# Wide weight loads for the small experts of a top-2-of-8 expert layer, and another order of the first loads

## The chip, the cores and the metric

The kernel runs on one core of one Trainium2 chip. Its time is the device time of one execution in microseconds, of the slowest core (here the only one): 1435.9 us is the median of three runs (1432.8 to 1438.07).

## The reference

A trunk of two layers over 256 tokens of 1024 columns, in float32. Each layer has three groups of attention heads beside each other (a 2-D neighbourhood, a dilated mixture, a fixed memory of 256 rows), an output projection and a channel mixer: a dense SwiGLU in layer 0, eight experts with the best two per token in layer 1.

```python
D_MODEL, SEQ, MEM_LEN = 1024, 256, 256
D_FF, N_EXPERTS, TOP_K, D_FF_EXPERT = 2816, 8, 2, 3584

def swiglu(x, w_gate, w_up, w_down):
    return (jax.nn.silu(x @ w_gate) * (x @ w_up)) @ w_down

# moe_swiglu, in short: each token goes through the two experts with the largest logits,
# and their results are added, weighted by a softmax over the two logits
logits = x @ w_router
top_logit, top_idx = lax.top_k(logits, TOP_K)
gates = jax.nn.softmax(top_logit, axis=-1)
y[token] += gate * swiglu(x[token], w_gate[e], w_up[e], w_down[e])
```

An expert has 29.36 MB of gate and up weights (1024 rows of 3584 columns each) and 14.68 MB of down weights (3584 rows of 1024 columns). All eight are read, whatever the routing.

## The kernel before

**Weights.** All weight loads stand in one list, `groups`, in the order in which they are used; SP alone issues them, through `fill` and `load` (L79). `fill` issues the next load as soon as a raw buffer is free, and it never passes one by. A raw buffer is 128 partitions of 2048 numbers, 1 MB. Up to the end of the dense part a load takes a whole buffer; the expert loads are 512 KB each and take half of one, so `fill` cuts whole buffers in two (`halves`). In the expert layer the halves are raw (6), rawm (10), rawu (4), rawlast (2) and rawh (1, of another size): 23 loads can be on their way or landed and unused at once. A chunk of an expert is 512 of its 3584 columns: eight loads of gate and up, each with two 2 KB rows per partition, and four loads of down rows of 4 KB, which come one chunk later.

**Experts by size.** Ranks are given after routing, by the number of tokens: `ids` holds which expert has which rank; numbers of experts below are these. Expert 0 is the one that is multiplied first, experts 1 and 2 are large, 3 to 7 small. `plan` is the order of the segments. A test on the token counts (`few > 32`) chooses between two copies of the rest of the program; the measured data take the second, straight one (L1275 to 1283), in which experts 3 to 7 have at most 32 tokens each.

**Large experts** (`split_segment`) need each weight as two numbers: ScalarE copies it to `whi` (L112), VectorE subtracts to `wlo` (L113), and TensorE multiplies three times (L192 to 194). The raw buffer is free after the subtraction. Expert 1 is done in seven pieces of one chunk each, with two tiles of tokens ("two").

**Small experts** (`small_segment`) multiply the raw weight itself: 32 columns of tokens against four column groups of TensorE (L973), the copy of the result (ScalarE), its turn by TensorE transposes (L990), Silu on ScalarE (L992), the product on VectorE (L993), and the down weights (L1018). A half buffer is free after its matmuls. At the end of a segment the result is taken apart into two numbers (L1009, L1011) and later added to the tokens (`combine`, L897 to 900).

**The straight block's order.** After expert 2 it runs the first four chunks of expert 7, expert 1's first piece, expert 7's other three chunks, expert 1's second piece, and so on through experts 6 and 5, then expert 3 with all chunks, expert 1's last piece, and expert 4. This makes seven turns from a small expert to a piece of expert 1 and to the next small one. Before each piece of expert 1 the first loads of the piece are split ahead; after each piece the first four loads of the small expert are split as well, and small_segment drops those splits (`spl.pop`) and takes the raw halves. Expert 4's last chunk loads its down weights as four column pieces (`down_columns`, `finish`, `store`), each of which ends in its part of the output.

**The start.** SP issues the first weight load (L79), one half of `mem` (L371), a second weight load, the other half of `mem`, more weights, and `x` (L374). POOL issues `gdil` and four loads of the position bias, `win` (L388 to 398), from its own queue, and adds `madd` to it later (L415). TensorE's first large work is on `mem`.

Of the kernel before, what the change touches and what calls it, by code (L numbers as in the profile page):

```python
# [13 lines left out]
ALU = mybir.AluOpType  # L14
# [26 lines left out]
def encoder_kernel(ctx: ExitStack, tc: tile.TileContext, a: dict, consts: bass.AP, out: bass.AP):  # L41
# [22 lines left out]
    pos_ = {"dma": 0, "split": 0, "use": 0, "end": 1 << 30, "most": 1 << 30}  # L64
# [17 lines left out]

    def halves(t):
        return [t[:, :1024], t[:, 1024:]]

    def fill(most=None):

        while pos_["dma"] < (most or len(groups)):
            i = pos_["dma"]
            if i >= n_dense and whole and not free:  # L90
                free.extend(halves(whole.pop(0)))
            room = whole if i < n_dense else free
            if not room:
                break
            t = room.pop(0)
            load(shaped(t, groups[i]), groups[i])
            if i < n_dense and sent:
                sent[0] = None
            raw[i] = t
            pos_["dma"] += 1  # L100

    def issue_split(engine=None):
# [13 lines left out]
        if any(t is x for x in once) and pos_["dma"] + len(free) >= n_dense + ONCE:  # L116
            pass
        elif i < pos_["end"]:
            (whole if i < n_dense else free).append(t)
            fill()  # L120
        else:
            raw[i] = t

    def next_group(ahead=None):
# [3 lines left out]
        while pos_["split"] < min(len(groups), i + 1 + ahead, pos_["most"]):  # L128
            issue_split()
# [12 lines left out]
    def released(i):  # L142
        free.append(raw.pop(i))
# [42 lines left out]

    NCH = DFE // 512
# [40 lines left out]
    def dense():  # L228
        st = ExitStack()
        with st:  # L230
# [118 lines left out]
            def attention_layer(l):  # L349
                with ExitStack() as sa:  # L350
# [12 lines left out]
                    if l == 0:  # L363
# [36 lines left out]
                    after_h = transposed(h, uh, ul, G_ATTN, l)  # L400
                    if l == 0:
                        mem_values(0, mh, ml)
# [255 lines left out]
    def moe():  # L658
        with ExitStack() as st:
# [387 lines left out]

            def result():
# [226 lines left out]
            with br.Else():  # L1275
# [3 lines left out]
                modes = ["two" if seg[0] == 1 else "one" if seg[0] == 2 else 32 for seg, _ in plan]  # L1279
                for i, (seg, after) in enumerate(plan[1:], 1):  # L1280
                    small_next = i + 1 < len(plan) and isinstance(modes[i + 1], int)
                    segment(seg, modes[i], before if seg[3] else [], after, not small_next)
# [76 lines left out]
```

## Time and profile before

| | |
|---|---|
| median of three runs | 1435.9 us |
| profiled execution, its own time | 1437.19 us |
| its span | 1435.4 us |
| granted clock, mean | 0.961 |
| TensorE busy | 1310.1 us (91%) |
| VectorE busy | 848.8 us (59%) |
| ScalarE busy | 679.5 us (47%) |
| GpSimd busy | 84.6 us (6%) |
| DMA | 428.09 MB, 298 GB/s over the span |

The span is what the profiler recorded from the first to the last instruction; the execution's own time holds 1.8 us around it. Busy shares are averages over stages with different limits: the dense layers come first, then expert 0, expert 2, and from 767 us on the straight block. So TensorE's 91% is no statement on any one of them, and the rows below look at stages, at one load, at one turn and at the start.

### The profile page before, as it was taken

Reading aid. Unit: us, or ns where it says so; the run is one execution under the profiler, and the core shown is the slowest. Engines: PE = TensorE matmul, PEld = TensorE weight load, DVE = VectorE, ACT = ScalarE, POOL = GpSimd, SP = SyncE. Lnnn points to the kernel's source line nnn. Section 1 sums busy time; section 2 is a strip of 40 time slices with the busy share of each in tenths; the row PEclk is TensorE's granted clock in tenths of the full one; section 3 lists DMA queues with packets and bytes.
Section 4 is the critical chain, followed back from the end, with each engine's and each line's share of the span. In section 5 each row is a group of like instructions: output and inputs, shape, how many; then the busy total and the mean of one; then the engine's idle time right before and its main releaser. Section 6 shows DMA issues by size and latency. Waiting matters only on the chain.

```text
span 1435.4 us, 23774 instructions
## 1 busy us (share of the span) xinstructions
PE 1310.1 (91%) x8669; PEld 966.3 (67%) x8669; DVE 848.8 (59%) x1431; ACT 679.5 (47%) x1060; POOL 84.6 (6%) x79
## 2 busy tenths in 40 slices
PE   6999999999999799999999898979897989758966
PEld 6886888888986578878886566637663757316523
DVE  5877877755986889979994444425442535005502
ACT  6676665643676477767773323223322333004201
POOL 0300011100201500000000000000000000000000
PEclk9999999999999999999999999989998999978989
DMA  8532455555744879779998999999999999999997
GB/s 244 177 122 80 159 191 179 185 197 155 213 151 155 313 266 368 275 273 352 366 370 306 395 386 392 356 396 371 395 373 396 382 396 372 394 396 390 366 395 281
DMA packets 208730, 428.09 MB, mean 298 GB/s; under 512 B 13420, under 2 KB 58036, under 8 KB 208596
## 3 DMA queue, kind: packets, MB, share of 16 engines
q1 hardware_dynamic: 207936, 424.89, 81.6%
q0 software_dynamic: 576, 1.48, 0.6%
q8 instruction: 72, 1.18, 0.3%
q14 instruction: 62, 0.51, 0.1%
q10 hardware_dynamic: 84, 0.04, 0.0%
HBM read 425.31 MB, written 1.05 MB: 297 GB/s over the span
## 4 chain that ended last, share of the span: by engine, by line
PE 72%; DMA 18%; DVE 5%; issue 2%; ACT 2%; SPq 0%; POOL 0%; ACTq 0%; DVEq 0%; POOLq 0%
PE gu L193 8%; PE gu L194 8%; PE gu L192 7%; PE acc L604 6%; PE gu L973 5%; DMA rawm<-in_w_down_moe_dram 4%; PE acc L192 3%; PE acc L193 3%; PE acc L194 3%; PE acc L605 3%; DMA rawm<-in_w_up_moe_dram 3%; DMA rawlast<-in_w_up_moe_dram 3%; PE y L193 3%; PE y L194 3%; PE y L192 3%
## 5 line engine op out<-in xcount | busy, mean ns | idle before, releaser
L113 DVE TENSOR_TENSOR wlo<-raw,whi 128x1024 fp32r<-128x1024 f32 (+2 forms) x193 | 220.4, 1147 | 84.0 <-ACT whi L112 81.2
L112 ACT ACTIVATE whi<-raw 128x1024 fp32r<-128x1024 f32 (+2 forms) x199 | 195.9, 994 | 113.2 <-PE acc L194 54.0
L192 PE MATMUL gu<-whi,x 128*128 128x512 f32 x358 | 147.3, 414 | 17.0 <-ACT whi L112 14.6
L193 PE MATMUL gu<-wlo,x 128*128 128x512 f32 x358 | 148.1, 414 | 6.1 <-DVE wlo L113 6.1
L194 PE MATMUL gu<-whi,x 128*128 128x512 f32 x358 | 146.8, 410 | 0.0
L113 DVE TENSOR_TENSOR wlo<-rawm,whi 128x1024 fp32r<-128x1024 f32 (+1 forms) x104 | 123.2, 1201 | 27.0 <-ACT whi L112 22.5
L604 PE MATMUL acc<-u,whi 128*128 128x512 f32 x352 | 124.7, 399 | 0.0
L112 ACT ACTIVATE whi<-rawm 128x1024 fp32r<-128x1024 f32 (+1 forms) x104 | 107.0, 1043 | 37.1 <-PE gu L194 25.0
L993 DVE TENSOR_TENSOR hs<-tr,hs 128x128 f32<-128x128 f32 x35 | 10.1, 289 | 187.1 <-ACT hs L992 187.1
L983 ACT COPY sg<-gu 128x256 f32<-128x256 f32 x35 | 13.0, 372 | 224.7 <-PE gu L973 221.5
L973 PE MATMUL gu<-rawm,xr 128*32 128x256 f32 x936 | 88.5, 398 | 13.3 <-DMA rawm<-in_w_up_moe_dram 9.4
L605 PE MATMUL acc<-u,wlo 128*128 128x256 f32 x352 | 98.9, 281 | 0.0
L192 PEld LDWEIGHTS gu<-whi,x 128*128 128x128 f32 x358 | 70.2, 198 | 36.4 <-ACT whi L112 17.8
L193 PEld LDWEIGHTS gu<-wlo,x 128*128 128x128 f32 x358 | 70.9, 198 | 25.8 <-DVE wlo L113 9.5
L194 PEld LDWEIGHTS gu<-whi,x 128*128 128x128 f32 x358 | 70.6, 197 | 16.5
L604 PEld LDWEIGHTS acc<-u,whi 128*128 128x128 f32 x352 | 66.2, 188 | 16.4
L192 PE MATMUL acc<-whi,u 128*128 128x384 f32 (+1 forms) x224 | 75.4, 336 | 1.4 <-ACT qk_dil L518 1.4
L193 PE MATMUL acc<-wlo,u 128*128 128x384 f32 (+1 forms) x224 | 74.7, 333 | 1.1 <-DVE wlo L113 1.1
L194 PE MATMUL acc<-whi,u 128*128 128x384 f32 (+1 forms) x224 | 74.5, 333 | 0.0
L973 PE MATMUL gu<-raw,xr 128*32 128x256 f32 x592 | 65.3, 413 | 9.7 <-DMA raw<-in_w_up_moe_dram 8.8
L973 PEld LDWEIGHTS gu<-rawm,xr 128*32 128x32 f32 x936 | 37.1, 112 | 44.4 <-DMA rawm<-in_w_up_moe_dram 15.6
L605 PEld LDWEIGHTS acc<-u,wlo 128*128 128x128 f32 x352 | 66.5, 189 | 0.0
(382 smaller groups left out, 2791.7 us busy)
## 6 DMA issues: line engine op xcount, KB each, us to landing
rawm<-in_w_down_moe_dram SPq DMA_DIRECT2D x98, 512.0 KB, 10.3
rawm<-in_w_up_moe_dram SPq DMA_DIRECT2D x95, 512.0 KB, 10.5
rawm<-in_w_gate_moe_dram SPq DMA_DIRECT2D x93, 512.0 KB, 10.5
raw<-in_w_gate_moe_dram SPq DMA_DIRECT2D x62, 512.0 KB, 10.3
raw<-in_w_down_moe_dram SPq DMA_DIRECT2D x61, 512.0 KB, 10.3
raw<-in_w_up_moe_dram SPq DMA_DIRECT2D x51, 512.0 KB, 10.6
rawu<-in_w_up_moe_dram SPq DMA_DIRECT2D x45, 512.0 KB, 6.7
rawu<-in_w_gate_moe_dram SPq DMA_DIRECT2D x37, 512.0 KB, 10.2
```

The source lines that it names most:

```text
L112: nc.scalar.activation(xh, x, AF.Copy)
L113: (engine or nc.vector).tensor_tensor(xl, x, xh.bitcast(F32), op=ALU.subtract)
L192: nc.tensor.matmul(ps, xh, wh, start=start, stop=False)
L193: nc.tensor.matmul(ps, xh, wl, start=False, stop=False)
L194: return nc.tensor.matmul(ps, xl, wh, start=False, stop=stop).ins
L604: nc.tensor.matmul(ps, wh[:, k, fs], u[:, k], start=k == 0, stop=False)
L605: nc.tensor.matmul(ps[:, 0, :], wl[:, k, fs], uh[:, k, :], start=False, stop=k == KT - 1)
L973: done = nc.tensor.matmul(ps[j * w:j * w + w, :], xr[:, k, :], v[m * half + (k - ks[0]) // 2][:, k % 2, c0:c0 + n], start=k == 0, stop=k = ...
L983: nc.scalar.copy(t, ps)
L993: nc.vector.tensor_tensor(s, pt[:, :, 64:], s, op=ALU.mult)
```

## The change

In the straight block, experts 3 to 7 work on halves of 1792 columns in place of chunks of 512. A gate or up load is now 128 partitions of one row of 1792 columns (7 KB), a down load 128 partitions of two rows of 1024 columns that lie behind one another in DRAM (8 KB); the last expert's last four down rows stay four column pieces of 512 KB. Such a load takes a whole raw buffer, so `fill` asks for a whole one, and `give` joins two free halves of one buffer again. A new `wide_segment` does the work: per half sixteen gate and up loads into two PSUM tiles of four column groups of 448 columns, Silu, one product, one block transpose on VectorE in place of ScalarE's copy and TensorE's transposes, and fourteen down rows. The first loads of a small expert are no longer split. Experts 7, 6 and 5 are cut in two halves each, so the number of turns is the same. At the start both halves of `mem` come ahead of the first weights, and `gdil` and `win` are issued for layer 0 by SP, behind three loads of w_in.

```diff
     def halves(t):
-        return [t[:, :1024], t[:, 1024:]]
+        res = [t[:, :1024], t[:, 1024:]]
+        joined.append((res, t))
+        return res
+
+    def give(t):
+        free.append(t)
+        if pos_["large"]:
+            for res, v in joined:
+                if any(t is x for x in res) and all(any(x is y for y in free) for x in res):
+                    free[:] = [y for y in free if not any(x is y for x in res)]
+                    whole.append(v)
+                    joined.remove((res, v))
+                    break
...
-            if i >= n_dense and whole and not free:
+            big = i < n_dense or math.prod(groups[i].shape[1:]) > 1024
+            if not big and whole and not free:
                 free.extend(halves(whole.pop(0)))
-            room = whole if i < n_dense else free
+            room = whole if big else free
...
+            j = pos_["split"]
+            if j >= n_dense and math.prod(groups[j].shape[1:]) > 1024:
+                break
             issue_split()
...
     def released(i):
-        free.append(raw.pop(i))
+        whole.append(raw.pop(i)) if math.prod(groups[i].shape[1:]) > 1024 else give(raw.pop(i))
         fill()
...
+    def wide_groups(e, parts, by_columns=False):
+        wg, wu = (a[nm][0, bass.ds(e, 1)].rearrange("e (k p) n -> p (e k) n", p=128)
+                  for nm in ("w_gate_moe", "w_up_moe"))
+        wd = a["w_down_moe"][0, bass.ds(e, 1)].rearrange("e (c p r) n -> p (e c) r n", p=128, r=WR)
+        res = []
+        for c in parts:
+            res += [w[:, k:k + 1, c * WIDE:(c + 1) * WIDE] for k in range(KT) for w in (wg, wu)]
+            ends = WR - 4 if by_columns and c == parts[-1] else WR
+            res += [wd[:, c, r:r + 2, :] for r in range(0, ends, 2)]
+            if ends < WR:
+                res += [wd[:, c, ends:, k:k + 256] for k in range(0, D, 256)]
+        return res
+
+    WIDE, WR = DFE // 2, DFE // 256
...
-                        fill(1)
                         for q in range(2):
                             nc.sync.dma_start(mt[:, :, q * 512:q * 512 + 512], mem_v[:, :, q * 512:q * 512 + 512])
-                            fill(2 + q)
+                            fill(1 + q)
+                        fill(3)
...
+                    after_h = transposed(h, uh, ul, G_ATTN, l)
+                    if l == 0:
+                        mem_values(0, mh, ml)
+
+                    queue = nc.sync if l == 0 else nc.gpsimd
                     gd = a["g_qk_dil"][l]
-                    nc.gpsimd.dma_start(gdil, bass.AP(tensor=gd.tensor, offset=gd.offset,
+                    queue.dma_start(gdil, bass.AP(tensor=gd.tensor, offset=gd.offset,
...
-                            nc.gpsimd.dma_start(win[i][par * 64:par * 64 + 64], bass.AP(
+                            queue.dma_start(win[i][par * 64:par * 64 + 64], bass.AP(
...
+                def down(s, r0, r1, first, last):
+                    for r in range(r0, r1):
+                        if r % 2 == 0:
+                            i, v = take_raw()
+                        for j in range(4):
+                            nc.tensor.matmul(y[j * 32:j * 32 + 32, :], s[:, r, :], v[:, r % 2, j * m:j * m + m],
+                                             start=first and r == 0, stop=last and r == r1 - 1)
+                        if r % 2:
+                            released(i)
+
+                for c in halfs:
+                    gu = [psum.tile([128, 512], F32, name="gu", bufs=2)[:, :n] for _ in range(2)]
+                    for k in range(KT):
+                        for ps in gu:
+                            i, v = take_raw()
+                            for j in range(4):
+                                done = nc.tensor.matmul(ps[j * 32:j * 32 + 32, :], xr[:, k, :],
+                                                        v[:, 0, j * n:j * n + n], start=k == 0, stop=k == KT - 1)
+                            released(i)
...
+                    t = mp.tile([128, 512], F32, name="sg", bufs=2)[:, :n]
+                    nc.scalar.activation(t, gu[0], AF.Silu)
+                    nc.vector.tensor_tensor(t, gu[1], t, op=ALU.mult)
+                    s = mp.tile([128, WR, 32], F32, name="hw", tag="th", bufs=2)
+                    nc.vector.transpose(s, t.rearrange("p (q r) -> p r q", r=WR))
...
+                    down(s, 0, WR - 4 if end else WR, c == halfs[0], c == halfs[-1])
...
+                pos_["large"] = True
+                plan[2:] = [((7, 1, [0], True), [(1, 0, 0), (1, CAP, 2)]),
+                            ((1, 0, [0], False), []),
+                            ((7, 1, [1], True), [(6, 0, 1)]),
...
```

At the start SP's list changes as follows; `mt` is mem and `raw_63` to `raw_65` are the weight buffers.

```order
+L405 DMA mt<-in_mem_dram 128x2x512
 L79 DMA raw_63<-in_w_mem_kv_dram 128x4x256
-L371 DMA mt<-in_mem_dram 128x2x512
+L405 DMA mt<-in_mem_dram 128x2x512
 L79 DMA raw_64<-in_w_mem_kv_dram 128x4x256
-L371 DMA mt<-in_mem_dram 128x2x512
 L79 DMA raw_65<-in_w_mem_kv_dram 128x8x256
```

Both halves of mem now stand ahead of the first two weight loads, which follow one behind the other. A few rows on, among the loads of w_in, stands what POOL's queue held before; `gdil` is the gain of the dilated heads, `win` the position bias.

```order
+L428 DMA gdil<-in_g_qk_dil_dram 128x128
 L79 DMA raw_63<-in_w_in_dram 128x4x384
+L436 DMA win_374<-in_rpb_na_dram 64x3x219
 L79 DMA raw_64<-in_w_in_dram 128x4x384
+L436 DMA win_374<-in_rpb_na_dram 64x3x219
+L436 DMA win_375<-in_rpb_na_dram 64x3x219 x2
 L79 DMA raw_65<-in_w_in_dram 128x4x384
```

One load of gdil and four of win are issued by SP, in front of the weight loads that come after them.

In the straight block SP's list, before, reads like this where expert 1's first piece ends and expert 7's remaining chunks begin; `rawu`, `rawm` and `raw` are buffers of which each row takes one half, and an `ISA` row behind each load is left out here.

```order
L79 DMA rawu<-in_w_down_moe_dram 128x1024
L79 DMA rawm_3422<-in_w_down_moe_dram 128x1024
L79 DMA rawm_3422<-in_w_gate_moe_dram 128x2x512
L79 DMA rawm_3423<-in_w_up_moe_dram 128x2x512
L79 DMA rawm_3423<-in_w_gate_moe_dram 128x2x512
L79 DMA raw_64<-in_w_up_moe_dram 128x2x512
L79 DMA raw_64<-in_w_gate_moe_dram 128x2x512
L79 DMA rawm_4715<-in_w_up_moe_dram 128x2x512
L79 DMA rawm_4715<-in_w_gate_moe_dram 128x2x512
```

Every 1 MB buffer stands in two rows that follow each other, one for each half. The same place after the change, again without the `ISA` rows, reads:

```order
L79 DMA rawm_3423<-in_w_gate_moe_dram 128x1792
L79 DMA raw_64<-in_w_up_moe_dram 128x1792
L79 DMA rawm_4715<-in_w_gate_moe_dram 128x1792
L79 DMA rawm_4716<-in_w_up_moe_dram 128x1792
L79 DMA rawm_4717<-in_w_gate_moe_dram 128x1792
L79 DMA raw_65<-in_w_up_moe_dram 128x1792
L79 DMA raw_63<-in_w_gate_moe_dram 128x1792
L79 DMA rawlast<-in_w_up_moe_dram 128x1792
L79 DMA rawu<-in_w_gate_moe_dram 128x1792
L79 DMA rawu<-in_w_up_moe_dram 128x1792
L79 DMA rawm_3422<-in_w_gate_moe_dram 128x1792
L79 DMA rawm_3423<-in_w_up_moe_dram 128x1792
```

Each row is a load of 128x1792 into a buffer of its own (`rawu` holds two), and the twelfth row takes the first row's buffer, `rawm_3423`, again: eleven buffers pass before one comes back.

## Rows read from the trace of the kernel before

**Rows 1.** The page's slices: one digit per 35.9 us, the DMA engines.

```profile
DMA  8532455555744879779998999999999999999997
```

**Rows 2.** Stages: window, length, busy us and counts per engine, clock, DMA share, GB/s.

```profile
757.00:767.00 10.00, 10.00 (x96) 7.39 (x98) 6.90 (x9) 4.96 (x7) 0.91 (x2) 1.00 0.30 93
767.00:1420.00 653.00, 563.82 (x4691) 352.91 (x4682) 239.63 (x312) 177.04 (x263) 11.12 (x14) 0.93 1.02 386
```

**Rows 3.** DMA view, 2 KB rows alone, 1240 to 1247 us.

```profile
DMA packets 1406, 2.71 MB, mean 387 GB/s; under 512 B 82, under 2 KB 82, under 8 KB 1406
```

**Rows 4.** DMA view, 4 KB rows alone, 1285 to 1290 us.

```profile
DMA packets 566, 2.06 MB, mean 411 GB/s; under 512 B 64, under 2 KB 64, under 8 KB 566
```

**Rows 5.** Timeline of SP in one turn: start us, us, what it issues.

```profile
903.20 0.37 SPq L79 DMA_DIRECT2D rawm<-in_w_gate_moe_dram  x1
913.16 0.37 SPq L79 DMA_DIRECT2D rawm<-in_w_up_moe_dram  x1
```

**Rows 6.** Timeline of TensorE and VectorE in the same turn.

```profile
869.36 1.05 PE L1018 MATMUL y<-raw,hs 128*32 128x256 f32 x16
...
874.97 0.80 PE L193 MATMUL gu<-wlast,x 128*128 128x512 f32 x1 [1.15 <-DVE wlast L113]
...
900.17 1.22 DVE L113 TENSOR_TENSOR wlo<-rawm,whi 128x1024 fp32r<-128x1024 f32 x1 [0.17 <-ACT whi L112]
...
910.46 1.23 DVE L113 TENSOR_TENSOR wlast<-rawm,wlast 128x1024 fp32r<-128x1024 f32 x1 [1.57 <-ACT wlast L112]
```

**Rows 7.** Chain of waits, 700 to 1436 us: start us, us, engine, out, line.

```profile
912.13 3.59 PE gu L973 x64
...
924.98 3.55 PE gu L973 x64
...
1408.37 0.73 PE y L1018 x8
```

**Rows 8.** Windows of the seven turns, and of the piece in one.

```profile
842.00:850.00 8.00, 8.00 (x84) 4.83 (x82) 4.72 (x7) 1.56 (x3) 1.60 (x2) 1.00 0.98 357
909.00:917.00 8.00, 8.00 (x85) 5.29 (x84) 4.21 (x6) 1.43 (x2) 1.60 (x2) 1.00 0.71 245
991.00:999.00 8.00, 8.00 (x84) 5.18 (x82) 4.11 (x6) 1.43 (x2) 1.55 (x2) 1.00 0.90 316
1057.00:1065.00 8.00, 8.00 (x84) 5.25 (x83) 4.09 (x7) 1.43 (x2) 1.60 (x2) 1.00 0.83 304
1139.00:1147.00 8.00, 8.00 (x83) 4.68 (x81) 5.23 (x8) 0.98 (x3) 1.55 (x2) 1.00 1.00 356
1204.00:1212.00 8.00, 8.00 (x85) 5.29 (x84) 4.16 (x6) 1.43 (x2) 1.60 (x2) 1.00 0.86 310
1333.00:1341.00 8.00, 8.00 (x81) 5.54 (x83) 5.97 (x8) 2.61 (x4) 1.61 (x2) 1.00 0.81 285
...
875.00:881.00 6.00, 6.00 (x14) 4.74 (x15) 4.73 (x5) 2.88 (x3) 0.00 (x0) 0.50 1.03 404
881.00:912.00 31.00, 31.00 (x137) 24.43 (x136) 16.11 (x16) 12.78 (x14) 1.19 (x2) 1.00 1.03 385
```

**Rows 9.** DMA view, whole span: one queue; one load (KB, us to landing).

```profile
q14 instruction: 62, 0.51, 0.1%
...
once<-in_w_gate_moe_dram SPq DMA_DIRECT2D x1, 512.0 KB, 3.6
```

**Rows 10.** Chain of waits, 0 to 100 us: mem's second half.

```profile
2.74 14.12 DMA mt<-in_mem_dram
```

**Rows 11.** DMA view of 7 to 15 us: all packets, and POOL's queue.

```profile
DMA packets 1139, 1.85 MB, mean 231 GB/s; under 512 B 103, under 2 KB 706, under 8 KB 1139
...
q0 software_dynamic: 257, 0.67, 40.7%
```

**Rows 12.** Timeline of POOL, 0 to 100 us.

```profile
37.79 7.78 POOL L415 TENSOR_TENSOR bias<-win,cd 128x384 f32<-128x384 f32 x6 [33.32 <-PE s L265]
49.58 1.86 POOL L536 TENSOR_TENSOR rp<-qk_dil,rope 128x768 f32<-128x768 f32 x1 [4.00 <-ACT qk_dil L518]
```

More of the change, by code (lines that the diff above doesn't have):

```diff
@@ L63, in encoder_kernel @@
     raw, spl, whole, free, once = {}, {}, list(raws), [], []
-    pos_ = {"dma": 0, "split": 0, "use": 0, "end": 1 << 30, "most": 1 << 30}
+    pos_ = {"dma": 0, "split": 0, "use": 0, "end": 1 << 30, "most": 1 << 30, "large": False}
     def wmat(ap, c0, n, kk=4):
@@ L1046, in small_segment, with wide_segment, take_raw @@
                 take_parts()
+            def wide_segment(seg, before, after):
+                col, slot, halfs, _ = seg
+                last_of_all = seg is plan[-1][0]
+                pos_["end"] = 1 << 30
+                n, m = WIDE // 4, 256
+                xr = mp.tile([128, KT, 64], F32, name="xr", tag="tl", bufs=2)[:, :, :32]
+                for q in range(2):
+                    ks = slice(q * 4, q * 4 + 4)
+                    nc.gpsimd.tensor_tensor(xr[:, ks, :], xs[slot][0][:, ks, :32].bitcast(F32),
+                                            xs[slot][1][:, ks, :32].bitcast(F32), op=ALU.add)
+                rows = [cm[:, 202 + j:203 + j] for j in range(4)]
+                y = psum.tile([128, 2, 512], F32, name="y", bufs=1)[:, 0, :m]
+                def take_raw():
+                    i = pos_["use"]
+                    pos_["use"] += 1
+                    pos_["split"] = pos_["use"]
+                    return i, shaped(raw[i], groups[i])
+                def down(s, r0, r1, first, last):
[8 more added lines that the diff above has]
+                for c in halfs:
+                    end = last_of_all and c == halfs[-1]
+                    gu = [psum.tile([128, 512], F32, name="gu", bufs=2)[:, :n] for _ in range(2)]
[6 more added lines that the diff above has]
+                            released(i)
+                        if end and k < KT - 1:
+                            busy(done.ins, 2, hg[:, 0, :T])
+                    t = mp.tile([128, 512], F32, name="sg", bufs=2)[:, :n]
[3 more added lines that the diff above has]
+                    nc.vector.transpose(s, t.rearrange("p (q r) -> p r q", r=WR))
+                    for col_, slot_, v in before[halfs.index(c):][:1]:
+                        if v:
+                            take(v)
+                        combine(col_, slot_, cb)
+                    if c == 0:
+                        turn_hot(one_hot(col, cm[:, :128], 32), phTs[slot])
+                    if c == halfs[-1]:
+                        for g in after:
+                            gather(*g, cb)
+                    down(s, 0, WR - 4 if end else WR, c == halfs[0], c == halfs[-1])
+                hi, lo = ([v.rearrange("p q c -> p (q c)")[:, j * m:j * m + m] for j in range(4)] for v in parts)
+                for j in range(4):
+                    nc.scalar.activation(hi[j], y, AF.Copy, scale=rows[j])
+                for j in range(4):
+                    nc.vector.scalar_tensor_tensor(lo[j], y, rows[j], hi[j].bitcast(F32), op0=ALU.mult,
+                                                   op1=ALU.subtract)
+                if last_of_all:
+                    combine(col, slot, cb)
+                    for c in range(4):
+                        i, v = take_raw()
+                        z = psum.tile([128, 512], F32, name="gu", bufs=2)[:, :256]
+                        for j in range(4):
+                            last = nc.tensor.matmul(z[j * 32:j * 32 + 32, :], s[:, WR - 4 + j, :], v[:, j, :],
+                                                    start=True, stop=True)
+                        released(i)
+                        finish(c, z, last.ins)
```

33 lines of the change are left out of this document (26 added, 7 removed).

## The prediction

> **What bounds the kernel now.** I read the page's header and its slices first, then the stages, then one load, one turn between experts and the start. The DMA line of the slices [rows 1] is at 9 from the middle of the span to its end; nothing before that is so even. The stages say it plainly: from 767 to 1420 us the DMA engines show a share of 1.02 and 386 GB/s, while TensorE is busy for 564 of 653 us, VectorE for 240 and ScalarE for 177 [rows 2]. So the straight block runs at the pace of its weights, 252 MB, and two things can shorten it: faster bytes, or fewer moments in which the queue has nothing to fetch.
>
> How fast a byte is depends on its row. A stretch with loads of 2 KB rows alone runs at 387 GB/s [rows 3], one with 4 KB rows alone at 411 GB/s [rows 4]. On each of 16 engines that is 84.7 ns for 2 KB and 159.5 ns for 4 KB: 74.8 ns for 2 KB more, so about 9.9 ns per row whatever its length.
>
> The queue runs empty at the turns. In the turn from expert 1's piece to the next small expert SP issues a load at 903.20 and the next at 913.16 [rows 5]: all 23 half buffers hold data that TensorE has not reached, because it works on expert 1 from 874.97 to 912.13 [rows 6, 7]. The seven turns have shares of 0.98, 0.71, 0.90, 0.83, 1.00, 0.86 and 0.81 over 8 us [rows 8]; against the 1.04 of a full stretch these are 9.5 us of idle queue, 1.4 per turn. A larger hole stands at 757 to 767, with a share of 0.30 [rows 2]: buffers full while expert 2's last matmuls run.
>
> **The change part by part, against the profiled execution's 1437.2 us (span 1435.4); the median of the runs is 1435.9, so 1.3 come off at the end.**
>
> *Wide rows.* For experts 7, 6, 5, 3 and 4 a load becomes 128 rows of 7 KB (gate, up) or 8 KB (down). The trace has no such weight load. With 9.9 ns per row and 36.5 ns per KB, 7 KB take 265.6 to 271.7 ns (the lower end without the fixed part growing at all, the upper from the line through 84.7 and 159.5) and 8 KB 309; I take the line, 422 and 424 GB/s. Bounds: 411 if longer rows bring nothing more, 430 without a fixed part. The instruction queue's packets are 0.51 MB in 62, so 8 KB in one piece does exist here [rows 9]. One expert has 29.36 MB of gate and up and 14.68 MB of down: before 75.9 + 35.7 = 111.6 us, after 69.6 + 34.6 = 104.2. Five experts: -37.0 us (bounds -22 and -42).
>
> The Trainium skill, "DMA: Bandwidth & Descriptors", section "Why small descriptors are slow (HBM only)", has a fixed cost of about three cycles per packet beside one cycle for 32 bytes. By that rule 2 KB and 4 KB rows would differ by 2.3%; the two stretches differ by 6.2%, so the measurement decides and the sum goes by the rows. With the rule's shape the five experts would win about 14 us, not 37, and the total would come out near no change, which is the time of rival (a) below.
>
> *Buffers.* The list of SP shows what the trace cannot: after the change a wide load needs a whole buffer, and eleven names pass before one comes again, where 23 halves did. Half buffer rawh and half of another stand empty then. 23 halves hold 12.06 MB, eleven gate or up tiles 10.09. First place: the hole at 757 to 767. The small expert's first weights come in under expert 2's matmuls; 1.97 MB fewer are there when it ends, 4.7 us at 422 GB/s. And the 10.09 MB that are hidden there save nothing: 26.1 - 23.9 = 2.2 us of the 37. Together +6.9 (bounds +5 and +9).
>
> Second place: the seven turns. From the landing of the last down load: its eight matmuls 0.7 us [rows 7]; from the end of y (869.36 + 1.05 = 870.41) to the first small matmul at 912.13, 41.7 us, in which the parts are taken, the first halves split, and expert 1's piece runs [rows 6, 7]; then the first wide tile, four matmuls of 448 columns. A small chunk's 64 records take 3.55 us for 8 rows of 1024 columns [rows 7], so one of 1792 columns takes 0.8. Only then is a buffer given back; until data flows again I estimate 1.3 us (an idle queue lands 512 KB in 3.6 us [rows 9], 1.36 of them transfer; bounds 0.5 and 2.2). Sum 44.5 us. The queue has work for 8 x 1.355 + 4 x 1.276 = 15.9 us (expert 1's halves) and 11 x 2.17 = 23.9 us (wide tiles): 39.8. So it idles 4.7 us per turn, 32.9 in seven, where it idled 9.5: +23.4 (bounds 0 and +35). This wait is in front of TensorE in no turn: it comes back as the end of the following expert's stream, which is behind by as much.
>
> *The block turn on VectorE.* Per small chunk of 512 columns ScalarE's copy, TensorE's two transposes, Silu and the product go; per half of 1792 columns Silu, product and one VectorE transpose of 448 columns stand instead. All lies beside seven down loads of 2.5 us each; VectorE is busy for 240 of 653 us. The four splits of halves that a small expert never used (the last starts at 910.46 [rows 6]) go too; TensorE is busy for all of 881 to 912 [rows 8], so nothing shortens. 0, bounds -2 and +2.
>
> *First loads.* mem goes ahead of the weights, and gdil and win leave POOL's queue for SP's, behind three loads of w_in. The second half of mem lands at 16.86 [rows 10]. From 7 to 15 us win's packets take 40.7% of the DMA engines' time [rows 11], 3.3 us, and the whole runs at 231 GB/s. TensorE needs both halves of mem and both first weight loads, 2.1 MB in either order, so it starts on the second half 3.3 us earlier, less a little for the weight's split, which now comes last: -3 (bounds 0 and -5). win on SP lands some 30 us in; POOL adds the bias at 37.79 for 7.78 us and has its next work at 49.58 [rows 12]: 4 us of cover. If that cover were gone, rope and the first attention would come later by what is over.
>
> *Tail.* The last loads are four column pieces of 512 KB as before. The last plain down load is followed by taking y and combining, some 4 us, beside four column loads of 1.4 us. Before, gate and up of the last chunk had their place there [rows 7]. 0, bounds -3 and +3.
>
> Sum: -37.0 + 6.9 + 23.4 + 0 - 3.0 + 0 = -9.7, so 1427.5, on the runs' median 1426.
>
> **The rivals.** (a) *Rows above 4 KB bring no more than 411 GB/s*, say because they are cut into pieces with a head each. Then an expert takes 107.2 us (-22.0 in five), a tile 2.23, the queue idles 4.0 per turn (+18.5), the first fill costs 6.3, the start gives 3: -0.2, so 1436. For it: the trace has no long row of weights; against it: the 8 KB instruction packets, and the even step from 2 to 4 KB. (b) *Slower: the ring is shorter than eleven.* A whole buffer is given back only when both of its halves are split. The twelfth half of expert 1 is split by 901.39 [rows 6], 31.7 us after the landing; the eleventh tile, which goes into its buffer, is wanted by 37.6, and issued 2 earlier: 4 us of room. Each tile less costs 2.17 us per turn. From an idle time of 7.1 us per turn on the change is slower by over 0.5%; with two tiles less it is 9.0, 63 in seven, and 1437.2 - 33.1 + 53.5 = 1457.6, on the median 1456. For it: SP issues in order, so one late buffer holds up all behind it, and TensorE works at half clock at each turn's start, 0.50 from 875 to 881 [rows 8]; if more of the piece ran so, the same would follow. (c) *The turns idle no longer than before*, 1.4 us each: then -33.1, 1404, on the median 1403. For it: two of the seven turns lose only 0.5 and 0.3 us now; against it: TensorE has no gap in the turn that could close.
>
> **How the numbers follow.** My forecast has 0.46, (a) 0.22, (b) 0.15, (c) 0.17. The bound for telling a change is 0.5%, 7.2 us: faster is below 1428.7, slower above 1443.1. The forecast's own range is 1419 to 1435; it lies below 1428.7 in 0.28 and within the bound in 0.18. (a) gives 0.02 to faster, 0.19 to the same and 0.01 to slower; all of (c) is faster, all of (b) slower. Faster 0.47, same 0.37, slower 0.16. The range of 1407 to 1448 leaves out half of (c) and seven tenths of (b), 0.19 together.
>
> **What would show it.** A stretch of wide loads at 415 GB/s or more shows the rows right, 411 or less (a). Seven holes of 4 to 5 us at the turns, each ended by the first wide tile's matmuls, show the ring; holes of 7 or more show (b), of under 2 (c). The second half of mem should land near 12 and what TensorE does with it come three us earlier than before. The prediction is wrong if the stage after 767 stops being bounded by the queue, or if the start's 3 us are gone by the end of the first layer.

## The result, and the profile after

The changed kernel takes 1451.5 us (median of 4 runs, 1448.6 to 1451.6); beside them the kernel before took 1435.7. The ratio is 1.0106 (95% interval 1.0083 to 1.0129), and in a second set of 5 runs 1.0110 (1.0091 to 1.0128). The change made the kernel slower by 1.1%, 15.8 us, where I forecast it 0.7% faster. Its span is 1449.2 us, against 1435.4.

The slices answer to [rows 1]: where a line of nines stood, eights come back at nearly equal distances.

```profile
DMA  8632555546645699879989989898989898999796
```

The stages, as in [rows 2] (window, length, busy us and counts by engine, clock, DMA share, GB/s):

```profile
767.00:1432.00 665.00, 553.30 (x3683) 310.69 (x3672) 209.53 (x266) 130.97 (x178) 6.15 (x14) 0.87 0.95 381
1432.00:1449.20 17.20, 13.53 (x68) 9.01 (x67) 6.91 (x14) 1.15 (x3) 0.00 (x0) 1.00 0.20 65
```

The share is 0.95 where it was 1.02. TensorE's busy time fell and so did VectorE's and ScalarE's: no engine became the bound. The queue is idle more. Where, the seven turns show, in windows that answer to [rows 8]:

```profile
831.00:841.00 10.00, 10.00 (x74) 5.88 (x76) 2.48 (x4) 0.00 (x0) 0.88 (x2) 1.00 0.41 146
906.00:916.00 10.00, 10.00 (x69) 6.23 (x71) 2.48 (x4) 0.00 (x0) 0.88 (x2) 1.00 0.36 131
983.00:993.00 10.00, 10.00 (x68) 6.14 (x70) 2.48 (x4) 0.00 (x0) 0.87 (x2) 1.00 0.27 88
1059.00:1069.00 10.00, 10.00 (x68) 6.13 (x70) 2.48 (x4) 0.00 (x0) 0.88 (x2) 1.00 0.35 124
1135.00:1145.00 10.00, 10.00 (x70) 5.97 (x73) 2.48 (x4) 0.00 (x0) 0.88 (x2) 1.00 0.36 126
1210.00:1220.00 10.00, 10.00 (x68) 6.07 (x70) 2.48 (x4) 0.00 (x0) 0.88 (x2) 1.00 0.39 143
1340.00:1350.00 10.00, 10.00 (x66) 6.42 (x68) 3.96 (x7) 1.26 (x2) 0.88 (x2) 1.00 0.18 53
```

A stream of wide loads has a share of 1.01 here (1.02 from 905 to 907 below). The seven shares are 0.60 to 0.83 short of it, over 10 us each: 47.5 us of lost queue, 6.8 per turn, against 9.5 before. That is +38.0 us, and the forecast had +23.4.

One turn of the changed kernel, mostly microsecond by microsecond:

```profile
905.00:907.00 2.00, 2.00 (x10) 1.61 (x9) 0.00 (x0) 0.00 (x0) 0.00 (x0) 1.00 1.02 419
907.00:908.00 1.00, 1.00 (x6) 0.80 (x5) 0.00 (x0) 0.00 (x0) 0.00 (x0) 1.00 0.89 366
908.00:909.00 1.00, 1.00 (x6) 0.82 (x5) 0.00 (x0) 0.00 (x0) 0.00 (x0) 1.00 0.26 108
909.00:910.00 1.00, 1.00 (x6) 0.82 (x5) 0.00 (x0) 0.00 (x0) 0.00 (x0) 1.00 0.09 36
910.00:914.00 4.00, 4.00 (x27) 2.25 (x30) 2.48 (x4) 0.00 (x0) 0.88 (x2) 1.00 0.00 0
914.00:915.00 1.00, 1.00 (x16) 0.39 (x12) 0.00 (x0) 0.00 (x0) 0.00 (x0) 1.00 0.56 129
915.00:916.00 1.00, 1.00 (x16) 0.37 (x12) 0.00 (x0) 0.00 (x0) 0.00 (x0) 1.00 0.78 258
```

The hole has three parts (shares against 1.01). From 907 to 910 the DMA engines run out, not all at once, 1.8 us of lost share; for 4 us nothing moves; from 914 to 916 the share comes back, 0.7 us lost. In the kernel before, the same turn stood still for one microsecond only, 913 to 914; the rest of its loss was running out and coming back:

```profile
911.00:912.00 1.00, 1.00 (x5) 0.56 (x3) 1.00 (x2) 0.00 (x0) 1.00 (x2) 1.00 0.69 248
912.00:913.00 1.00, 1.00 (x21) 0.60 (x24) 1.00 (x3) 0.00 (x0) 0.41 (x2) 1.00 0.19 70
913.00:914.00 1.00, 1.00 (x24) 0.60 (x20) 1.00 (x2) 0.00 (x0) 0.00 (x0) 1.00 0.01 2
914.00:915.00 1.00, 1.00 (x24) 0.63 (x20) 0.08 (x1) 0.00 (x0) 0.00 (x0) 1.00 0.78 115
```

SP's issues in that turn of the changed kernel answer to [rows 5] (timeline; the eleven from 877.11 to 901.84 are the wide tiles of the next small expert):

```profile
877.11 0.33 SPq L79 DMA_DIRECT2D rawlast<-in_w_gate_moe_dram  x1
...
886.24 0.33 SPq L79 DMA_DIRECT2D rawm<-in_w_up_moe_dram  x1
892.01 0.33 SPq L79 DMA_DIRECT2D rawm<-in_w_gate_moe_dram  x1
900.44 0.33 SPq L79 DMA_DIRECT2D raw<-in_w_up_moe_dram  x1
901.84 0.33 SPq L79 DMA_DIRECT2D raw<-in_w_gate_moe_dram  x1
913.52 0.33 SPq L79 DMA_DIRECT2D rawlast<-in_w_up_moe_dram  x1
```

TensorE's instructions there answer to [rows 6, 7]:

```profile
870.35 1.94 PE L1111 MATMUL y<-rawm,hw 128*32 128x256 f32 x16 [1.51 <-DMA rawm<-in_w_down_moe_dram]
...
876.85 0.80 PE L228 MATMUL gu<-wlo,x 128*128 128x512 f32 x1 [0.66 <-DVE wlo L129]
...
912.48 0.96 PE L1123 MATMUL gu<-rawlast,xr 128*32 128x448 f32 x8
```

All eleven tiles are issued by 901.84; the twelfth goes out at 913.52, behind the first matmuls on a wide tile (912.48). TensorE has the last down load at 870.35, the first product with a `wlo` only at 876.85.

A stretch with 7 KB rows alone and one with 8 KB rows alone (DMA view) answer to [rows 3, 4]. First 7 KB:

```profile
DMA packets 1106, 7.09 MB, mean 417 GB/s; under 512 B 118, under 2 KB 118, under 8 KB 1104
```

And the 8 KB rows:

```profile
DMA packets 537, 3.96 MB, mean 417 GB/s; under 512 B 55, under 2 KB 55, under 8 KB 55
```

417 GB/s in both, where I took 422 and 424. At the start, mem's two halves land 6.0 us after their issue, where the second took 14 [rows 10]; by the timelines the first small matmul comes at 761.56, where it came at 763.77. The loads of mem in the DMA view (KB, us to landing):

```profile
mt<-in_mem_dram SPq DMA_DIRECT2D x2, 512.0 KB, 6.0
```

From 7 to 15 us, where win's packets stood [rows 11], the DMA view now has

```profile
DMA packets 2015, 3.02 MB, mean 377 GB/s; under 512 B 77, under 2 KB 1614, under 8 KB 2015
```

and POOL's timeline, which answers to [rows 12], shows the bias begun 3 us earlier than before, when win has landed from SP's queue, and POOL's next work right behind it, so that the cover of 4 us is used up:

```profile
34.80 9.14 POOL L452 TENSOR_TENSOR bias<-win,cd 128x384 f32<-128x384 f32 x6 [34.34 <-DMA win<-in_rpb_na_dram]
43.91 1.82 POOL L573 TENSOR_TENSOR rp<-qk_dil,rope 128x768 f32<-128x768 f32 x1
```

The lead is not constant. By VectorE's timelines the changed kernel is 6.0 us ahead at 62 us, 4.8 from 74 us to 500 us, and 2.2 from 650 us on: over two of it go where expert 2 begins.

Last the tail, which the forecast had at nothing. TensorE's timeline (L1111 multiplies the down loads, L1155 the column pieces, L777 is explained below):

```profile
1427.97 1.07 PE L1111 MATMUL y<-rawu,hw 128*32 128x256 f32 x16 [1.50 <-DMA rawu<-in_w_down_moe_dram]
...
1432.38 0.62 PE L1155 MATMUL gu<-rawm,hw 128*32 128x256 f32 x2
1432.93 1.13 PE L777 MATMUL y<-hg 128*128 128x256 f32 x4
...
1434.13 1.12 PE L777 MATMUL y<-hg 128*128 128x256 f32 x4
...
1440.38 1.03 PE L777 MATMUL y<-hg 128*128 128x256 f32 x4
1441.34 0.64 PE L1155 MATMUL gu<-rawm,hw 128*32 128x256 f32 x8
```

L777 is `busy`: dummy matmuls that keep TensorE from standing still while it waits for weights. The kernel before has some too (L740). They write the PSUM tile `y`. Before, `y` is read ahead of the last chunk's gate and up, so its dummies run among those. `wide_segment` issues fourteen for the last half (two records each), but there `y` is not read until the last plain down load is through: they run from 1432.93 on, some between the combining matmuls, and the third column piece waits until 1441.34.

### The profile page after: what moved, and what is told of

The parts are those of the page before. It is cut to its first block, busy times and chain, and to the rows that moved or that the text cites. A ratio compares the mean times of both kernels' runs of the same rounds, so it can differ in the third digit from the quotient of the medians.

```text
span 1449.2 us, 20752 instructions
## 1 busy us (share of the span) xinstructions
PE 1307.8 (90%) x7655; PEld 930.3 (64%) x7655; DVE 816.5 (56%) x1384; ACT 628.9 (43%) x968; POOL 77.7 (5%) x74
## 4 chain that ended last, share of the span: by engine, by line
PE 71%; DMA 20%; DVE 4%; issue 2%; ACT 2%; SPq 0%; POOL 0%; ACTq 0%; DVEq 0%; POOLq 0%
PE gu L228 8%; PE gu L229 7%; PE gu L227 7%; PE acc L641 6%; DMA rawm<-in_w_gate_moe_dram 5%; DMA rawm<-in_w_down_moe_dram 5%; PE gu L1123 5%; PE acc L227 4%; PE acc L228 4%; PE acc L229 4%; PE acc L642 3%; PE y L229 3%; PE y L228 3%; PE y L227 3%; DMA rawu<-in_w_down_moe_dram 3%
## 5 line engine op out<-in xcount | busy, mean ns | idle before, releaser
L129 DVE TENSOR_TENSOR wlo<-raw,whi 128x1024 fp32r<-128x1024 f32 (+2 forms) x183 | 208.9, 1147 | 66.9 <-ACT whi L128 66.4
L128 ACT ACTIVATE whi<-raw 128x1024 fp32r<-128x1024 f32 (+2 forms) x189 | 185.5, 991 | 93.1 <-PE acc L229 58.0
L227 PE MATMUL gu<-whi,x 128*128 128x512 f32 x370 | 153.1, 417 | 20.7 <-ACT whi L128 18.0
L229 PE MATMUL gu<-whi,x 128*128 128x512 f32 x370 | 151.5, 409 | 0.0
L129 DVE TENSOR_TENSOR wlo<-rawm,whi 128x1024 fp32r<-128x1024 f32 (+1 forms) x89 | 105.5, 1198 | 23.8 <-ACT whi L128 22.9
L128 ACT ACTIVATE whi<-rawm 128x1024 fp32r<-128x1024 f32 (+1 forms) x89 | 91.6, 1040 | 39.0 <-PE gu L229 30.1
L227 PEld LDWEIGHTS gu<-whi,x 128*128 128x128 f32 x370 | 73.0, 199 | 42.3 <-ACT whi L128 22.9
L228 PEld LDWEIGHTS gu<-wlo,x 128*128 128x128 f32 x370 | 73.4, 198 | 27.8 <-DVE wlo L129 11.2
L1123 PE MATMUL gu<-rawm,xr 128*32 128x448 f32 x616 | 77.6, 610 | 10.9 <-DMA rawm<-in_w_up_moe_dram 5.8
L1147 DVE SCALAR_TENSOR_TENSOR yl<-y,cm,yh 128x256 fp32r<-128x256 f32 x32 | 13.3, 478 | 122.8 <-ACT yh L1145 122.8
L641 PEld LDWEIGHTS acc<-u,whi 128*128 128x128 f32 x352 | 66.2, 188 | 16.4
L1130 DVE TENSOR_TENSOR sg<-gu,sg 128x448 f32<-128x448 f32 x10 | 6.2, 624 | 115.6 <-PE gu L1123 115.6
L937 DVE SCALAR_TENSOR_TENSOR h<-cb,gateS,h 128x512 f32<-128x512 f32 x44 | 31.8, 748 | 64.7 <-PE cb L935 64.7
L1145 ACT ACTIVATE yh<-y,cm 128x256 fp32r<-128x256 f32 x32 | 12.5, 474 | 127.1 <-PE y L1111 127.1
```

The costliest lines, as they stand in the source:

```text
L128: nc.scalar.activation(xh, x, AF.Copy)
L129: (engine or nc.vector).tensor_tensor(xl, x, xh.bitcast(F32), op=ALU.subtract)
L227: nc.tensor.matmul(ps, xh, wh, start=start, stop=False)
L228: nc.tensor.matmul(ps, xh, wl, start=False, stop=False)
L229: return nc.tensor.matmul(ps, xl, wh, start=False, stop=stop).ins
L641: nc.tensor.matmul(ps, wh[:, k, fs], u[:, k], start=k == 0, stop=False)
```

## The experiments

Each was run beside the kernel before, whose median was 1436.6 us in the first set, 1434.5 in the second and 1435.6 in the third. My theory after the result: the turns and the dummies are the loss, the rows do what they should. Rivals: long rows bring nothing; the new start costs; the holes come from the queue itself and not from the ring and TensorE. Sums over the seven turns are worked out as above, from seven windows against a share of 1.01 (1.02 with short rows). Times of different sets are compared as they stand; by the ratios the differences change by 1.5 us at most.

**No dummies.**

```diff
-                        if end and k < KT - 1:
-                            busy(done.ins, 2, hg[:, 0, :T])
```

> The changed kernel (1451.5 us) without the fourteen dummy matmuls that its wide segment issues for the last half of the last expert. They write the PSUM tile y and so cannot run before y has been read, which is after the last plain down load; in the trace of the changed kernel they stand at 1432.93 to 1441.3, ahead of the last two column matmuls. Theory (the tail lost 4.5 us to them: from the last landing to the end 17.7 us, before 13.2): 1447, bounds 1444 and 1449.5. Rival (the tail is longer because combine and the taking of y stand there, the dummies only fill a wait): 1451.5.

Measured 1442.4 us, ratio 1.0042 (1.0022 to 1.0062): 9 us less, more than the 4.5 expected and outside my bounds. The pair of kernels further down that differ by the dummies alone differ by 5.0 us. TensorE's timeline without them has the last plain down load at

```profile
1426.71 1.07 PE L1111 MATMUL y<-rawu,hw 128*32 128x256 f32 x16 [1.49 <-DMA rawu<-in_w_down_moe_dram]
```

and the span ends at 1442.1, 15.4 us later; with them it is 21.2 us (1427.97 to 1449.2). So in the traces they cost 5.8 us; by the times it is 9 in one pair and 5 in the other.

**The old start.** Weights before mem, `win` and `gdil` on POOL's queue again, issued where they stood before.

```diff
+                        fill(1)
                         for q in range(2):
                             nc.sync.dma_start(mt[:, :, q * 512:q * 512 + 512], mem_v[:, :, q * 512:q * 512 + 512])
-                            fill(1 + q)
-                        fill(3)
+                            fill(2 + q)
...
-                    queue = nc.sync if l == 0 else nc.gpsimd
+                    queue = nc.gpsimd
```

> The changed kernel with the order of the first loads as before (weights first, win and gdil on POOL's queue). Theory (the new start gives 2.2 us: the first small matmul came at 761.6 in place of 763.8): 1453.7. Rival (the new start costs something that later stages hide in the comparison): 1451.5 or less.

Measured 1452.8 us, ratio 1.0122 (1.0100 to 1.0144). The direction is as expected, but the interval holds the changed kernel too: by time alone the new start is worth something between nothing and 3 us. In this run the first small matmul comes at 763.17, in the changed kernel at 761.56. The traces of all runs say more: with the old start (three) it comes at 762.9 to 763.8, on average 763.3, with the new one (ten) at 757.9 to 762.3, on average 760.7, so 2.6 us earlier. Some 70 us in, at VectorE's first `kk`, the averages are 73.4 and 68.8, 4.5 us apart.

**Splits first.** The loads stay; only the program has two splits of expert 1's piece ahead of the taking of `y`.

```diff
+                if at < len(plan) and plan[at][0][0] == 1:
+                    for _ in range(2):
+                        issue_split()
...
                 for j in range(4):
                     nc.scalar.activation(hi[j], y, AF.Copy, scale=rows[j])
```

> The changed kernel, with the first two splits of expert 1's piece ahead of the taking of y on ScalarE and VectorE at each of the seven turns. Nothing of the loads changes. Theory (each turn's hole lasts until TensorE has done expert 1's piece, so an earlier start of the piece closes it by as much): the first wlo comes about 2.9 us earlier, seven turns give 20 us, 1431, bounds 1428 and 1438; the holes shrink from 6.9 to 4. Rival (the hole is the length of the queue, eight loads in flight, or the last engines' drain, whatever TensorE does): 1451.5 with holes of 6.9.

Measured 1442.0 us, ratio 1.0040 (1.0028 to 1.0052): 9.4 us less, half of what I expected and outside my bounds. ScalarE's timeline shows why:

```profile
869.48 0.84 ACT L1149 ACTIVATE yh<-y,cm 128x256 fp32r<-128x256 f32 x2 [15.87 <-PE y L1111]
870.21 1.05 ACT L128 ACTIVATE whi<-rawh 128x1024 fp32r<-128x1024 f32 x1
871.15 0.84 ACT L1149 ACTIVATE yh<-y,cm 128x256 fp32r<-128x256 f32 x2
```

Two of the four copies of `y` still stand ahead of the first split: the scheduler took them first. The seven turns now sum to 37.3 us of lost queue, 10.2 less, and the time fell by 9.4. From TensorE's first matmul on the last down load to its first on a wide tile it is 41.3 us on average over the seven turns, 42.7 in the changed kernel; seven times the difference, 1.35, is 9.4 too. The rival, for which TensorE's start has no say, falls.

**Ring of ten.** One 1 MB buffer is dropped the first time its halves are joined (`drop` starts at 1).

```diff
...
-                    whole.append(v)
+                    if pos_["drop"]:
+                        pos_["drop"] -= 1
+                    else:
+                        whole.append(v)
```

> The changed kernel with one raw buffer of 1 MB taken out of circulation in the straight block, so ten whole tiles in place of eleven. Theory (the ring's bytes set how long the queue has work while TensorE is on expert 1): one tile of 0.92 MB is 2.2 us per turn, 15.7 in seven, and 2.2 at the first hole: 1469, holes of about 9. Rival (the ring's length isn't what empties the queue): 1451.5.

Measured 1467.9 us, ratio 1.0219 (1.0197 to 1.0240): 16.4 us more, where 17.5 were expected. The holes are too wide here for windows of 10 us; in windows of 22 us the seven turns lose 60.1 us, in the changed kernel 47.7: 12.4 more, or 1.8 per turn, where 15.7 were expected. TensorE is no slower (42.3 to 44.3 us from the last down load to the first wide tile, 41.9 to 44.7 in the changed kernel), but in that time 14.6 to 14.9 MB are moved, in the changed kernel 15.4 to 15.7: one tile less. So the length of the ring sets the hole.

**Short rows.** The same buffers and matmuls, each wide load as two DMAs.

```diff
-            load(shaped(t, groups[i]), groups[i])
+            v, g = shaped(t, groups[i]), groups[i]
+            if i >= n_dense and big:
+                b, w = g.shape[1:]
+                for u in range(2):
+                    cut = (slice(None), slice(u, u + 1)) if b == 2 else (slice(None), slice(None), slice(u * w // 2, (u + 1) * w // 2))
+                    load(v[cut], g[cut])
+            else:
+                load(v, g)
```

> The changed kernel with each wide load issued as two: 896 columns (3.5 KB rows) for gate and up, one row of 1024 columns (4 KB) for down, into the same buffers and used in the same way. Theory (long rows do what was forecast, about 9 us per expert against 2 KB rows; the loss is elsewhere): by the packets of both traces, 3.5 KB take about 144.9 ns against half of 280.4, and 4 KB 163.6 against half of 315.1, so +2.4 and +1.3 us per expert, +18.6 in five; the seven holes shrink by 0.8 each since eleven tiles take longer, -6: 1464, bounds 1458 and 1470. Rival (long rows bring the stream nothing, and so the change lost its gain there): 1451.5.

Measured 1460.5 us, ratio 1.0175 (1.0156 to 1.0195): 9 us slower than with long rows, below the 12.5 expected, inside the bounds. A stretch of 3.5 KB rows:

```profile
DMA packets 1996, 6.47 MB, mean 404 GB/s; under 512 B 222, under 2 KB 222, under 8 KB 1995
```

404 GB/s against 417. The seven turns sum to 37.7 us, 9.8 less, so the rows themselves cost nearly 19 us more, as the packets had it (by the rates of the stretches, 404 and 411 against 417, it would be 14). Long rows work; the rival falls. The holes shrank by 1.4 per turn where 0.8 were expected from the slower stream; whether the smaller loads give the rest was not tried.

**The piece early.** The first two loads of expert 1's piece go ahead of the last down load, and are split ahead of its matmuls.

```diff
-            i = pos_["dma"]
+            i = dorder.get(pos_["dma"], pos_["dma"])
...
+                        down(s, 0, WR - 2 * LATE, c == halfs[0], False)
+                        pos_["split"] = pos_["use"] + LATE
+                        for _ in range(FIRST):
+                            issue_split()
+                        down(s, WR - 2 * LATE, WR, False, True)
...
+                        seq = list(range(g1, g1 + FIRST)) + list(range(g1 - LATE, g1))
+                        dorder.update(zip(range(g1 - LATE, g1 + FIRST), seq))
...
+    FIRST, LATE = 2, 1
```

> The changed kernel with the first two loads of expert 1's piece ahead of the small expert's last down load, at each of the seven turns, and their two splits ahead of that load's matmuls; the same loads, buffers and matmuls otherwise. Theory (a hole lasts until TensorE has done the piece; moving the two splits alone gave 1.5 us per turn): now TensorE can go from the last down matmul straight to the piece, 4 us earlier than in the changed kernel, 28 in seven: 1423, bounds 1418 and 1432, holes of about 3. Rival (the other part of the hole, the drain of the DMA engines one by one, can't be closed so, or SP is late): holes of 5 and 1438.

Measured 1430.5 us, ratio 0.9970 (0.9956 to 0.9983): 21 us less than the changed kernel, and the seven turns sum to 27.0 us, 20.5 less. What the turns gain, the end gains. It fell short of 28, inside the bounds. TensorE's timeline shows an order that I had not expected:

```profile
865.89 1.94 PE L1111 MATMUL y<-rawm,hw 128*32 128x256 f32 x16 [1.50 <-DMA rawm<-in_w_down_moe_dram]
868.33 1.22 PE L227 MATMUL gu<-whi,x 128*128 128x512 f32 x2 [0.51 <-ACT whi L128]
...
873.59 1.07 PE L1111 MATMUL y<-raw,hw 128*32 128x256 f32 x16
```

The piece's first matmuls (868.33) now run ahead of those on the last down load (873.59), since the scheduler placed them so.

**Both together**, early pieces and no dummies.

> The two together: expert 1's first two loads and splits early, and no dummy matmuls at the end. Theory (two separate losses, turn and tail, that add): 9 us below the kernel with early pieces alone, 1415, so faster than the kernel before the change by 1.4%. Rival (the tail's dummies keep the clock up for what follows, or the two overlap): 1423 or more.

Measured 1425.5 us, ratio 0.9937 (0.9923 to 0.9950): 5.0 us less than with the dummies. That is 10.5 us above the expected 1415: 7.5 of it are the early piece's own shortfall (1430.5 for 1423), the rest the dummies, 5.0 where the two expectations leave 8. By the number it lies where the rival had it, 1423 or more. The traces speak for adding all the same: from the last plain down load to the end it is 21.6 us with early pieces and 15.3 with early pieces and no dummies, a difference of 6.3, and 5.8 without early pieces. **Earlier still** is the same with `FIRST, LATE = 4, 2`:

> As the one before, with four loads and splits of the piece ahead of the last two down loads. Theory (once the piece starts directly behind the last down matmul, more does not help, TensorE sets the hole): 1415, the same as with two. Rival (the clock falls at the turn because TensorE waits on the down loads there; with more of the piece ready the first matmuls are not held up by splits either): 1408.

Measured 1416.4 us, ratio 0.9870 (0.9855 to 0.9885), the fastest kernel of this study: by the ratios 1.3% faster than before the change and 2.3% faster than after it. The time is near the expected 1415, but the theory behind that number, that four loads give no more than two, is refuted: it is 9.1 us below the kernel with two. Whether the clock has a part in it, as the rival had it, was not tried. Three of its seven turns:

```profile
829.00:839.00 10.00, 10.00 (x77) 5.17 (x76) 2.48 (x4) 0.00 (x0) 0.88 (x2) 1.00 0.88 338
902.00:912.00 10.00, 10.00 (x76) 5.16 (x75) 2.67 (x5) 0.00 (x0) 0.88 (x2) 1.00 0.67 258
...
1314.00:1324.00 10.00, 10.00 (x77) 5.41 (x79) 3.69 (x6) 1.26 (x2) 0.88 (x2) 1.00 0.70 269
```

The seven sum to 18.6 us of lost queue, 8.4 less than the 27.0 of `2, 1`; the time fell by 9.1. **Three down loads behind the piece**, `FIRST, LATE = 4, 3`, goes too far:

> Wide, no dummies, with the piece's first four loads ahead of the last three down loads in place of two. Theory (what is left is 2.7 us per turn, of which about 2 are the engines' drain and the first landing; one more down load behind the piece gives TensorE up to 1.2 us more per turn): 1411, bounds 1407 and 1416. Rival (SP is late by then, or the splits wait for their loads in any case): 1416.4 as with two.

Measured 1431.9 us, ratio 0.9975 (0.9963 to 0.9986). I had not named this way of losing. ScalarE's timeline:

```profile
864.04 1.06 ACT L128 ACTIVATE wlast<-rawm 128x1024 fp32r<-128x1024 f32 x1 [0.25 <-DMA rawm<-in_w_gate_moe_dram]
...
878.20 1.57 ACT L1151 ACTIVATE yh<-y,cm 128x256 fp32r<-128x256 f32 x4 [1.62 <-PE y L1111]
879.64 2.02 ACT L128 ACTIVATE whi<-rawm 128x1024 fp32r<-128x1024 f32 x2
```

Four splits are done by 865.1; the fifth stands behind the taking of `y` (878.20), which waits for the last down load. From 875 to 885 TensorE is busy for 6.85 of 10 us. The turns sum to 32.5 us.

**The kernel before, with early pieces** (four loads ahead of four down loads of 512 KB, the same bytes as with `4, 2`; the order of the loads is changed as above).

```diff
...
+                if dorder and plan[at][0][0] == 1:
+                    for _ in range(FIRST):
+                        issue_split()
                 down(s, len(chunks) == 1, True)
...
+    FIRST, LATE = 4, 4
```

> The kernel before the change, with the first four loads of expert 1's piece ahead of the small expert's last four down loads (the same bytes as two wide ones) and their splits ahead of the matmuls of these, at each turn. Theory (an early piece only fills idle queue, and before the change the turns hold 8.4 us of it): 1429, bounds 1426 and 1434. Rival (an early piece shortens TensorE's way, whatever the queue does, so it gives here too what it gave after the change): 1410.

Measured 1429.6 us, ratio 0.9961 (0.9946 to 0.9976), as expected: 6.1 us, where [rows 8] had 9.5 to give. Its turns have shares like this:

```profile
901.00:909.00 8.00, 8.00 (x84) 5.29 (x83) 4.49 (x6) 1.23 (x2) 1.60 (x2) 1.00 1.03 397
...
1126.00:1134.00 8.00, 8.00 (x72) 5.67 (x74) 5.68 (x7) 2.04 (x2) 1.55 (x2) 1.00 0.98 374
```

So an early piece helps only as far as there is idle queue. With early pieces on both sides, the wide loads, the new start and the tail without dummies are worth 13 us together (1429.6 to 1416.4), although the wide kernel's turns still lose 18.6 us and these under 1.

**The changed kernel again.** 

> The changed kernel once more, on the chip of these runs. Both theories: 1451, ratio 1.011.

 Measured 1451.4 us, ratio 1.0110.

## Why the prediction was wrong, step by step

| step | forecast, us | measured, us | from |
|---|---|---|---|
| long rows, five experts | -37.0 | -30.0 | 44.04 MB at 417 GB/s: 105.6 per expert, before 111.6 |
| first fill | +6.9 | +6.5 | 1.9 MB fewer before the first small matmul, and 10.09 MB at the old rate |
| seven turns | +23.4 | +38.0 | 47.5 of lost queue, 9.5 before |
| start | -3.0 | -2.2 | first small matmul at 761.56, not 763.77 (on average over all traces -2.6) |
| tail | 0 | +4.5 | lost share in the last 45 us: 13.8 (against 1.01), before 9.3 (against 1.04) |

The sum is +16.8; the medians differ by 15.8, the two profiled executions by 14.3.

The first fill shows in the rates: in the 100 us ahead of the first small matmul 335 GB/s are moved, before 354, which is 1.9 MB less, 4.6 us at 417 GB/s. The hole there is no longer than it was (7.1 us of lost share, before 7.4). The bytes are missing ahead of it, from 723 to 753 us, where SP issues the eleven tiles 3 us apart, as whole buffers come free, and a tile takes 2.2.

**The step that failed is the second place of the ring's term, the seven turns: the 39.8 us for which the queue was to have work.** The other side of that subtraction was right. From TensorE's first matmul on the last down load (870.35 in the turn above) to its first on a wide tile I had 42.4 us, and it is 41.9 to 42.8 in six turns and 44.7 in the last; data flows again after 43.9 to 44.8 us (46.7 in the last), where I had 44.5. But the 39.8 us are twelve halves and eleven tiles, 16.4 MB, all of them still to be moved when the last down load has landed. The seven turns move 15.4 to 15.7 MB in that time, 36.8 to 37.6 us at 417 GB/s: 0.7 to 1.0 MB had been moved before. That is about 2 us per turn and 14 in seven; the turns lost 47.5 us where the forecast had 32.9, 14.6 more. The 4.7 us that I was left with are near the time in which nothing, or next to nothing, moves (4 us in the turn above). The loss has running out and coming back besides, 1.8 + 0.7 us there, and the 9.5 us of the kernel before, against which I set it, are nearly all of that kind. Why those bytes run ahead of the landing was not looked at.

**The second failure is the tail.** I named taking `y` and combining and gave it bounds of 3 us; that the dummies write `y` and would have to wait for it I did not see, though the changed program shows it: `busy` takes the one PSUM tile `y`, and `wide_segment` reads `y` only behind the last plain down load. Without them the tail costs nothing, as forecast: the last 45 us lose 7.8 us of share, before 9.3.

**Right or nearly:** the rate of long rows, inside its bounds, its gain 7 us smaller; the first fill; the count of eleven; that a hole ends with the first wide tile. The start is right in its sum by luck: the new order gave 4.5 us some 70 us in, more than the 3.0 forecast, and about 2 of it went later, in the profiled pair where expert 2 begins (VectorE's timeline has 4.6 us of lead at 627 and 2.2 at 650). One price of the prediction does not fit its own line: 36.5 ns per KB is 37.4 for a KB of 1024 bytes, so the 265.6 ns and the bound of 430 GB/s are slips, and with 430 the far bound would be -46, not -42; the sum does not use them. The rule that I had weighed against the rows, from the Trainium skill, "DMA: Bandwidth & Descriptors", section "Why small descriptors are slow (HBM only)", would by my estimate have had long rows win 14 us; the measurement disagrees with it, at 30. Of the rivals, (a), rows worth no more than 411, is half true: 417 lies midway between that and my 422 to 424, and so does the gain of 30 between 22 and 37. But rows of 3.5 and 4 KB are 9 us slower than those of 7 and 8; by the rates most of that is the step from 3.5 to 7 KB. (b) came nearest in time, 1456, but not by its mechanism: the ring is not shorter than eleven. The late buffer that it named exists, SP waits from 892.01 to 900.44 for a split, yet the queue has a share of 1.02 at 905 to 907; it costs nothing there. Its other leg, TensorE at half clock for more of the piece, is not seen either: the granted clock is 0.50 from 870 to 879, before from 875 to 881 [rows 8], and from the end of `y` to the first small matmul it is 40.2 us, before 41.7. My own sign (holes of 4 to 5 us for the ring, of 7 or more for (b)) decides nothing, with 6.8. (c), turns as short as before, is what early pieces come near to: 18.6 us.

What stays open: the dummies' price is 6 us in the traces but 5 and 9 in the times; the terms add up to 1 to 2.5 us more than was measured; and why the last turn is the longest (share 0.18) is known only so far, that TensorE takes 44.7 us there.

## What to carry to other kernels

Larger loads pay by the row and charge by the ring: count in bytes what the buffers hold while the engine that frees them is elsewhere, less what has been moved before it leaves, and compare it with that time, lost share with lost share. If it falls short, let the next piece's first loads and its first preparation go ahead of the last loads of the piece before, up to the point where something else waits behind that preparation. And filler work needs a place to write: look at what its destination waits for.

## What the runs showed of the hardware

A queue that empties costs more than its pause: the DMA engines end over some 3 us (shares of 0.89, 0.26 and 0.09 in one us each) and take 2 us to come back (0.56, 0.78). Rates by row, each in a stretch of its own: 387 GB/s at 2 KB, 404 at 3.5, 411 at 4, 417 at 7 and at 8; above 4 KB longer rows bring 1.5%.
